# Decay and rate products on the array's two row halves, an own buffer for the short chunk's values, other orders at both ends, and PSUM scratch for inverses and decode

## The chip, the cores and the metric

The program runs on one core of a Trainium2 chip. The time is device microseconds from the launch to the end of one execution. Before the change it was 2742.42 us, the median of three runs (2741.14 to 2746.84).

## The reference

One inference step of a two-layer decoder: 16 meta tokens plus 1024 prompt tokens, and 8 further sequences with one token each, 1048 tokens in all, model width 1024. Layer 0 mixes tokens with a Conformer convolution, layer 1 with RWKV-7; each is followed by a squared-ReLU MLP of width 4096. Cut to what the change touches:

```python
def _rwkv7(h, shift_prev, S0, ...):                       # layer 1
    r = xr @ w_r; k = xk @ w_k; v = xv @ w_v              # xr.. = h + (previous h - h) * x_mix[i]
    w_log = -softplus(-(w0 + tanh(xw @ w1) @ w2)) - 0.5   # w1: 1024 x 64, w2: 64 x 1024: the decay
    decay = exp(-exp(w_log))
    a = sigmoid(a0 + (xa @ a1) @ a2)                      # a1: 1024 x 64, a2: 64 x 1024: the rate
    g = sigmoid(xg @ g1) @ g2
    # scan over the tokens, per head (64 x 64 state):
    #   sa = S @ -kk;  S = S * decay + sa (kk a)^T + v k^T;  y = S @ r
    out = ((group_norm(y) + bonus) * g) @ w_o
def _trunk(...):
    h = h + mixer(rmsnorm(h))                             # per layer
    h = h + square(relu(rmsnorm(h) @ w_mlp_in)) @ w_mlp_out
    return rmsnorm(h), conv buffers, shift rows, states   # the last 30 rows of each conv input are an output
```

## The kernel before

Activations lie with channels on the 128 partitions, eight blocks of 128 channels (KT = 8) by tokens. The tokens are cut into three groups of about 350 columns. Large products run in three passes: a weight is loaded as f32 (`pg_raw`), ScalarE casts it to `pg_hi` (L157), GpSimd subtracts to `pg_lo` (L162), and `mm3` (L187 to L189) adds hi\*hi, lo\*hi and hi\*lo. The RWKV projections (L891) are plain f32 matmuls, each of which shows as two records.

**Start.** `transpose_x` (L463) loads a group of x, squares and sums it on ScalarE (L437), takes the root (L438), transposes x (L470), and multiplies x by a diagonal matrix of 1/rms (L486, result `tn`). ScalarE (L488, `hn_h`) and VectorE (L489, `hn_l`) turn `tn` into the split activations, with norm weights from `pvec`, which `load_vecs` (L442) fills with small DMAs, a transpose and a copy (L453). `pw1` (L493) loads and splits the first conv weights (`pg`, `pa`) and multiplies (`ps_g`). Eight DMAs on ScalarE's queue (L1640) copy the old conv rows from one DRAM tensor to another.

**RWKV front.** Per group of tokens, `narrow` forms `p_wa`, in whose first 64 rows the decay's narrow product lies and in whose last 64 the rate's. `decay_rate` (L971) writes them to two 128-row tiles `lw` and `la` whose other halves hold constants (L807 to L809), and per head pair `lora2` (L981) multiplies the full 128 rows twice: `l_w` and `l_a` (L983). Values `vv` are transposed to `vt` (L1023, L1025) and written to DRAM (`d_v`, L1026). In the first group the 16 meta tokens, a short chunk, go the same way through `vm` (L1029, L1030), a tile with the same buffer tag as `vt`.

**Recurrence.** 17 chunks of 64 tokens. For a group of chunks `inverses` (L1159) loads blocks from DRAM into `ni`, runs 30 pairs of a product `tt` (L1172) and an add into `ni` (L1173) on VectorE, and writes them to DRAM (`d_p`). A chunk's `front` (L1186) loads `p` from there, transposes it to `x` on VectorE (L1203), and multiplies `A` (L1209), 64-row matmuls in pairs at `tile_position=(64 * q, 0)`. `chunk` (L1246) then begins with `gg` (L1257), which needs `x`, and `bT` (L1275).

**After the recurrence's first chunks.** Group 0's output projection (`ps_oo`, weights `wo`), its MLP (`m_h` L284, `m_l` L285, `ps_in`, `out`), the last chunks, and `norm_gate` for the later groups are interleaved. `filler` hands out generators by points: each `yield n` of a filling generator holds it back n points of the main stream. In this stage TensorE's instructions run in the order in which they are written (`in_order`); elsewhere the tile framework's scheduler orders every engine. `decode_step` (L1375) updates the states of the 8 single-token sequences on VectorE in 16 slices (`Sdec`, L1406 to L1414) beside group 0's MLP.

```python
nc.vector.tensor_mul(t4, S, overv(2))                             # L1406
nc.vector.tensor_reduce(sa[:, vs], t4, axis=AX.X, op=ALU.add)     # L1407
nc.vector.tensor_mul(S, S, overv(0))                              # L1408
nc.vector.tensor_mul(t4, overk(sa[:, vs]), overv(3))              # L1409
nc.vector.tensor_add(S, S, t4)                                    # L1410
nc.vector.tensor_mul(t4, overk(dq[:, 5, vs]), overv(1))           # L1411
nc.vector.tensor_add(S, S, t4)                                    # L1412
```

**End.** `final(g)` (L1552) squares the eight blocks, adds them into two tiles `acc_f` on GpSimd and VectorE (L230), sums over the channels with a matmul by ones (`fs`, L1569), transposes (`pf`, L1585), scales (L1588, L1590) and stores.

## Time and profile before

The profiled execution took 2743.3 us, of which the span between its first and last instruction is 2741.6 us: 1.7 us lie around it.

| what | us |
|---|---|
| median of three runs | 2742.42 |
| the profiled execution | 2743.3 |
| its span | 2741.6 |
| TensorE (PE) idle, total | 110.6 |
| VectorE (DVE) busy | 1727.8 |
| GpSimd (POOL) busy | 1455.6 |
| ScalarE (ACT) busy | 1124.0 |

The idle time is the span less the 2631.0 us in which PE was busy. A row of the timeline gives the start in us, the length of the stretch, the engine, the line, the operation, the output and inputs, shapes and the number of instructions in it; in brackets the idle time ahead of it and what ended it. A row of the windows gives, for a stretch of the span, its length and the busy time and count of each engine, then the granted TensorE clock (1.00 is full), DMA share and GB/s. A row of groups gives the line, operation, count, and after the bar the busy time and the mean ns of one.

### The profile page before, as it was taken

How to read it: one execution, taken by the hardware profiler on the slowest of the kernel's cores; microseconds unless marked ns; L12 is line 12 of the kernel's file. 1: busy time of each engine (PE TensorE's matmuls, PEld its weight loads, DVE VectorE, ACT ScalarE, POOL GpSimd, SP SyncE). 2: the span in 40 equal slices, each digit the busy share in tenths (PEclk: the TensorE clock that was granted, in tenths of full speed). 3: DMA queues.
4: the chain of work that ended last, by engine and by line, in shares of the span. 5: the costliest groups of instructions: out<-in, count | busy, mean ns of one | idle time of the engine just before them, and what ended most of it. 6: DMA issues, size and time to landing. Idle time of an engine off the chain costs nothing. (4 is left out here: it accounts for less than half of the span.)

```text
span 2741.6 us, 51590 instructions
## 1 busy us (share of the span) xinstructions
PE 2631.0 (96%) x19876; PEld 2489.7 (91%) x19876; DVE 1727.8 (63%) x3552; ACT 1124.0 (41%) x2097; POOL 1455.6 (53%) x2060
## 2 busy tenths in 40 slices
PE   8999999999999999998999999869998999999998
PEld 7999999999999999787887787768998999999998
DVE  5999999997445445335657466576679754334445
ACT  5546445445444333332434444434543542222223
POOL 6677878878887775022111113455677663333331
PEclk9999999999999999999999999989999999999999
DMA  6663544554456443667777768776675642222211
GB/s 182 170 185 113 163 138 125 158 174 131 142 159 192 138 139 101 184 198 198 202 189 203 189 166 196 192 192 163 176 234 165 166 130 87 66 69 70 70 55 43
DMA packets 624389, 412.30 MB, mean 150 GB/s; under 512 B 121656, under 2 KB 567288, under 8 KB 624142
## 3 DMA queue, kind: packets, MB, share of 16 engines
q1 hardware_dynamic: 543228, 358.60, 46.9%
q10 hardware_dynamic: 72386, 24.56, 4.2%
q0 software_dynamic: 8528, 25.83, 2.9%
q8 instruction: 157, 2.57, 0.4%
q14 instruction: 90, 0.74, 0.1%
HBM read 345.76 MB, written 64.07 MB: 149 GB/s over the span
## 5 line engine op out<-in xcount | busy, mean ns | idle before, releaser
L162 POOL TENSOR_TENSOR wo_lo<-wo_raw,wo_hi 128x256 fp32r<-128x256 f32 x736 | 546.7, 777 | 316.0 <-ACT wo_hi L157 314.2
L162 POOL TENSOR_TENSOR wi_lo<-wi_raw,wi_hi 128x256 fp32r<-128x256 f32 x640 | 472.1, 772 | 252.9 <-ACT wi_hi L157 244.4
L187 PE MATMUL out<-hh,wo_hi 128*128 128x352 f32 (+2 forms) x1536 | 501.5, 326 | 21.8 <-DVE h L354 12.8
L187 PE MATMUL ps_in<-m_h,wi_hi 128*128 128x352 f32 (+2 forms) x1536 | 494.3, 322 | 1.1 <-DVE h L354 1.1
L188 PE MATMUL out<-hh,wo_lo 128*128 128x352 f32 (+2 forms) x1536 | 495.2, 322 | 0.0
L189 PE MATMUL out<-hl,wo_hi 128*128 128x352 f32 (+2 forms) x1536 | 494.2, 322 | 0.0
L354 DVE TENSOR_TENSOR h<-h,out 128x352 f32<-128x352 f32 (+2 forms) x768 | 385.5, 510 | 171.7 <-PE out L189 170.1
L189 PE MATMUL ps_in<-m_l,wi_hi 128*128 128x352 f32 (+2 forms) x1536 | 492.2, 321 | 0.7 <-DVE m_l L285 0.7
L188 PE MATMUL ps_in<-m_h,wi_lo 128*128 128x352 f32 (+2 forms) x1536 | 491.8, 320 | 0.0
L524 DVE SCALAR_TENSOR_TENSOR cv<-u,wdw,cv 128x352 f32<-128x352 f32 (+2 forms) x720 | 377.8, 572 | 0.8
L157 ACT CAST wo_hi<-wo_raw 128x1024 fp32r<-128x1024 f32 x184 | 192.9, 1048 | 340.1 <-PE out L189 175.2
L157 ACT CAST wi_hi<-wi_raw 128x1024 fp32r<-128x1024 f32 x160 | 167.8, 1049 | 396.4 <-PE out L189 180.4
L187 PEld LDWEIGHTS out<-hh,wo_hi 128*128 128x128 f32 x1536 | 291.9, 190 | 27.9 <-DVE h L354 14.7
L188 PEld LDWEIGHTS out<-hh,wo_lo 128*128 128x128 f32 x1536 | 291.6, 190 | 0.8
L187 PEld LDWEIGHTS ps_in<-m_h,wi_hi 128*128 128x128 f32 x1536 | 289.4, 188 | 2.7 <-issue 1.3
L189 PEld LDWEIGHTS out<-hl,wo_hi 128*128 128x128 f32 x1536 | 290.5, 189 | 0.0
L189 PEld LDWEIGHTS ps_in<-m_l,wi_hi 128*128 128x128 f32 x1536 | 288.6, 188 | 1.9 <-DVE m_l L285 1.3
L188 PEld LDWEIGHTS ps_in<-m_h,wi_lo 128*128 128x128 f32 x1536 | 288.7, 188 | 0.9
L342 DVE SCALAR_TENSOR_TENSOR ps_in<-ps_in,rs_m 128x352 f32<-128x352 f32 (+2 forms) x192 | 100.2, 523 | 241.0 <-PE ps_in L189 240.6
L141 DVE TENSOR_TENSOR hl<-ps_in,hh 128x352 fp32r<-128x352 f32 (+2 forms) x192 | 98.6, 514 | 117.8 <-ACT hh L140 117.8
L343 ACT ACTIVATE ps_in<-ps_in 128x352 f32<-128x352 f32 (+2 forms) x192 | 85.0, 443 | 135.0 <-DVE ps_in L342 134.8
L1052 POOL DMA_DIRECT2D d_n<-n x32 | 24.6, 768 | 211.3 <-DVE n L1042 141.7
(361 smaller groups left out, 4823.3 us busy)
## 6 DMA issues: line engine op xcount, KB each, us to landing
wi_raw<-in_w_mlp_in_dram SPq DMA_DIRECT2D x160, 512.0 KB
wo_raw<-in_w_mlp_out_dram SPq DMA_DIRECT2D x160, 512.0 KB
wk_raw<-in_rwkv_w_k_dram SPq DMA_DIRECT2D x32, 512.0 KB
wr_raw<-in_rwkv_w_r_dram SPq DMA_DIRECT2D x32, 512.0 KB
wv_raw<-in_rwkv_w_v_dram SPq DMA_DIRECT2D x32, 512.0 KB
d_ab<-ab POOLq DMA_DIRECT2D x32, 512.0 KB, 4.6
pg_raw<-in_conv_w_pw_dram SPq DMA_DIRECT2D x24, 512.0 KB
pa_raw<-in_conv_w_pw_dram SPq DMA_DIRECT2D x24, 512.0 KB
```

The lines of the kernel that those rows point to most:

```text
L141: eng_lo.tensor_sub(lo, src, hi.bitcast(F32))
L157: nc.scalar.copy(hi[:, :a * b], raw[:, :a * b])
L162: eng_lo.tensor_sub(lo[:, cs], raw[:, cs], hi[:, cs].bitcast(F32))
L187: nc.tensor.matmul(ps, w[0], act[0], start=first, stop=False)
L188: nc.tensor.matmul(ps, w[1], act[0], start=False, stop=False)
L189: nc.tensor.matmul(ps, w[0], act[1], start=False, stop=last)
L342: nc.vector.scalar_tensor_tensor(s, s, 0.0, rs()[:, :n], op0=ALU.max, op1=ALU.mult)
L343: nc.scalar.activation(s, s, AF.Square)
L354: nc.vector.tensor_add(hv[:, 4 * i + m, :], hv[:, 4 * i + m, :], ps[:, :n])
L524: nc.vector.scalar_tensor_tensor(acc[m][:, :n], ug[:, m, j:j + n], wdw[:, m, j:j + 1], acc[m][:, :n], op0=ALU.mult, op1=ALU.add)
L1052: nc.gpsimd.dma_start(d_n[ch0:ch0 + ncg, p].rearrange("c r t -> r c t"), n32[:, :ncg])
```

## The change

The diff cut to what does work (arguments that only hand things through are left out):

```diff
+        nc.scalar.activation(eps_t[:, 3:4], eps_t[:, 0:1], AF.Sqrt)
...
             def transpose_x(g, ah, al, between=lambda: None):
                 n = G0[g][1]
+                staged = stage_vecs(0) if g == 0 else None
                 tiles = load_x(xin, g)
...
                 if g == 0:
-                    load_vecs([0])
+                    place_vecs(0, staged)
+                between()
...
+                    nc.sync.dma_start(o_conv_sample[0, m, 0:CB - 1, :], sd[m // 4][m % 4 * CB + 1:(m % 4 + 1) * CB])
...
-                for _ in transpose_x(0, *acts[0]):
-                    pass
+                first = pw1_weights(0, 0)
+                with tc.manual_schedule(engines={nc.scalar.engine}):
+                    for _ in transpose_x(0, *acts[0], lambda: ready.append(next(first))):
+                        pass
+                    ready.append(next(first))
...
-        lwa = [lorap.tile([P, N1], F32, name=f"l{b}") for b in "wa"]
-        for i, t in enumerate(lwa):
-            nc.scalar.copy(t[HALF[1 - i]], hsel[HALF[1 - i], 0:1].broadcast_to([HS, N1]))
+        lwa = lorap.tile([P, N1], F32, name="lwa")
...
-                        vm = pr.tile([P, 2, P], F32, name=nm("vm", p), tag="vt")
+                        vm = pr.tile([P, 1, P], F32, name=nm("vm", p), tag="vm")
...
-                for i, (t, b, nb, sign) in enumerate(((cum, "w", "w0", 0.5), (nav, "a", "a0", -0.5))):
-                    pl = lora2(wa2, p, lwa[i], f"{b}{p}")
+                pls = [bank(nm("l2", f"{b}{p}")) for b in "wa"]
+                for i, pl in enumerate(pls):
+                    nc.tensor.matmul(pl[:, :n], wa2[HALF[i], p, :], lwa[HALF[i], :n], start=True, stop=True, tile_position=(HS * i, 0))
+                for pl, t, nb, sign in zip(pls, (cum, nav), ("w0", "a0"), (0.5, -0.5)):
...
+            aside = bank(f"tt{c}", "x")[:B] if c + n == NCH else None
...
-                o = wk.tile([P, 256], F32, name=f"tt{c}_{j}", tag="tt")[:B, :j * wd].rearrange("p (s t) -> p s t", t=wd)
+                o = aside if aside is not None else wk.tile([P, 256], F32, name=f"tt{c}_{j}", tag="tt")[:B]
+                o = o[:, :j * wd].rearrange("p (s t) -> p s t", t=wd)
...
+        HOLD = 8
...
+            if c == NCH - 4:
+                yield HOLD
...
-                    t4 = rows(dk.tile([P, HV * HS], F32, name=f"t4{hv}", tag="t4"))
+                    t4 = rows(bank(f"t4{hv}", "x")[:, :HV * HS])
...
-                accs = mean_parts(hv, n, f"f{g}", True, "facc")
-                yield 3
+                if g:
+                    accs = [(actp, actp2)[g - 1].tile([P, cur["wide"]], F32R, name=f"fq{g}{k}", tag=f"acth{k}").bitcast(F32)
+                            for k in range(KT)]
+                else:
+                    accs = mean_parts(hv, n, f"f{g}", True, "facc")
+                    yield 3
                 for k in range(KT):
+                    if g:
+                        nc.scalar.activation(accs[k][:, :n], hv[:, k, :], AF.Square)
...
-                        nc.tensor.matmul(ps[:w, j:j + 1], acc[:, i:i + w], ones_d[:, 0:1], start=q == 0, stop=q == 1)
+                        nc.tensor.matmul(ps[:w, j:j + 1], acc[:, i:i + w], ones_d[:, 0:1], start=q == 0, stop=q == len(accs) - 1)
...
-                    if np_:
-                        nc.sync.dma_start(o_y_prompt[0, c:c + np_, :], ot[:np_, :])
+                        if np_:
+                            nc.sync.dma_start(o_y_prompt[0, c:c + np_, cs], ot[:np_, cs])
...
-            DL, DN = 74, 90
+            DL, DN, NL = 74, 90, 16
...
-                                ([late_start(DL), decode_step()], DL + DN), ([norm_gates(GN_OF[1]), ng2], NGA))
+                                ([late_start(DL), decode_step()], DL + DN), ([late_start(NL), norm_gates(GN_OF[1]), ng2], NGA + NL))
...
-            for q in range(DEC):
-                nc.scalar.dma_start(o_conv_sample[0, q, 0:CB - 1, :], state_conv[0, q, 1:CB, :])
```

So: the small vectors' loads are issued before those of x; a root is computed at the program's start, so that its table is loaded there; the first group's ScalarE work runs in written order, with the first `pg` split ahead of `hn_h` and the first `pa` split behind it; the eight DRAM copies are replaced by eight stores from tiles on chip, issued on SyncE's queue in the conv stage. Decay and rate sit in one tile `lwa`, and each pair of products is two 64-row matmuls at row positions 0 and 64 into two PSUM banks. `vm` has its own tag. The last group's `tt` and decode's `t4` lie in PSUM banks. Chunk 13 is held back by 8 points between its front and its first product, and the later norm gates start 16 points later. In the last two groups the squares go into the ones matmul without the adds, 24 matmuls a group for 6, and the outputs are stored by column halves.

ScalarE at the start, in the first group's `transpose_x`; `xj` is the squared x, `ss` its root, `hn_h` the split activation, `pg_0`, `pa_0`, `pg_1` conv weights. Before:

```order
L437 ACTIVATE xj_2_153,ss_2_154<-xt_2_151 96x1024
L157 CAST pg_0_hi<-pg_0_raw 128x1024
L1640 DMA out_dram<-in_state_conv_dram 16x1856 x2
L438 ACTIVATE ss_2_154<-ss_2_154,eps_t 96x1
L157 CAST pa_0_hi<-pa_0_raw 128x1024
L1640 DMA out_dram<-in_state_conv_dram 16x1856 x2
L157 CAST pg_1_hi<-pg_1_raw 128x1024
L1640 DMA out_dram<-in_state_conv_dram 16x1856
L488 ACTIVATE hn_h<-tn_0_216,pvec 128x352
L488 ACTIVATE hn_h<-tn_1_222,pvec 128x352
L488 ACTIVATE hn_h<-tn_2_228,pvec 128x352
```

After the change (line numbers are those of the changed kernel):

```order
L439 ACTIVATE ss_2_168<-ss_2_168,eps_t 96x1
L158 CAST pg_0_hi<-pg_0_raw 128x1024
L496 ACTIVATE hn_h<-tn_0_228,pvec 128x352
L496 ACTIVATE hn_h<-tn_1_234,pvec 128x352
L496 ACTIVATE hn_h<-tn_2_240,pvec 128x352
L496 ACTIVATE hn_h<-tn_3_246,pvec 128x352
L496 ACTIVATE hn_h<-tn_4_252,pvec 128x352
L496 ACTIVATE hn_h<-tn_5_258,pvec 128x352
L496 ACTIVATE hn_h<-tn_6_264,pvec 128x352
L496 ACTIVATE hn_h<-tn_7_270,pvec 128x352
L158 CAST pa_0_hi<-pa_0_raw 128x1024
L158 CAST pg_1_hi<-pg_1_raw 128x1024
```

All eight `hn_h` stand ahead of the casts of `pa_0` and `pg_1`, and the DRAM copies are gone.

TensorE where group 0's output projection is interleaved with chunk 13: `ps_oo0_6` and `ps_oo0_7` are its last two blocks, `ps_in1_0_0` to `ps_in1_2_0` the MLP's first three, `gg13` and `bT130` chunk 13's first products. Before:

```order
L188 MATMUL ps_oo0_6_20121<-z0_h7_19656,wo0_6_lo_19959 128x328
L189 MATMUL ps_oo0_6_20121<-z0_l7_19664,wo0_6_hi_19958 128x328
L1257 MATMUL gg13_20149<-x3213_19921,no13_19775 32x32 x16
L1275 MATMUL bT130_20173<-ident_58,bk13_19770 128x128 x4
L1275 MATMUL bT131_20179<-ident_58,bk13_19770 128x128 x4
L187 MATMUL ps_oo0_7_20189<-z0_h0_19649,wo0_7_hi_20064 128x328
```

After the change; the rows left out are the rest of `ps_oo0_7`, the statistics of the norm and the MLP's first three blocks:

```order
L190 MATMUL ps_oo0_6_20079<-z0_l7_19644,wo0_6_hi_19927 128x328
L188 MATMUL ps_oo0_7_20107<-z0_h0_19629,wo0_7_hi_20027 128x328
...
L189 MATMUL ps_in1_2_0_20267<-m10_h7_20142,wi1_0_2_lo_20259 128x328
L190 MATMUL ps_in1_2_0_20267<-m10_l7_20150,wi1_0_2_hi_20258 128x328
L1279 MATMUL gg13_20301<-x3213_19890,no13_19755 32x32 x16
L1297 MATMUL bT130_20325<-ident_58,bk13_19750 128x128 x4
L1297 MATMUL bT131_20331<-ident_58,bk13_19750 128x128 x4
L188 MATMUL ps_in1_3_0_20346<-m10_h0_20135,wi1_0_3_hi_20339 128x328
```

`gg13` has moved behind 100 more matmuls of 328 columns.

ScalarE at the last head pair of the first RWKV group: `vt0_7` and `vm0_7` are the transposed values of the long and the short chunks, `d_v` their place in DRAM, `r161` the key norm whose root it takes. Before:

```order
L1025 COPY vt0_7_13682<-vt0_7_13681 128x256
L979 ACTIVATE lg1_13626<-lg1_13626 128x256
L1026 DMA d_v_75<-vt0_7_13682 128x2x128
L1029 COPY vm0_7_13688<-vt0_7_13681 16x128
L921 ACT_TABLE_LOAD
L921 ACTIVATE r161_13756<-r161_13756 128x256
L1030 DMA d_v_75<-vm0_7_13688 16x128
L1067 COPY rk21_0_13782<-pr1_0_13743 128x256
```

After the change, where `sv` is the recurrence's first load of values from `d_v`:

```order
L1040 COPY vt0_7_13691<-vt0_7_13690 128x256
L1044 COPY vm0_7_13697<-vt0_7_13690 16x128
L994 ACTIVATE lg1_13635<-lg1_13635 128x256
L1041 DMA d_v_76<-vt0_7_13691 128x2x128
L1045 DMA d_v_76<-vm0_7_13697 16x128
L1262 DMA sv_12379<-d_v_76 64x8x64
L936 ACT_TABLE_LOAD
L936 ACTIVATE r161_13765<-r161_13765 128x256
```

The copy to `vm` now stands right behind that to `vt`, both stores follow, and a load from `d_v` has come ahead of the table load.

42 lines of the change are left out of this document (25 added, 17 removed).

## The prediction

> **What bounds the kernel now.** I read the busy shares first, then busy time by stage, then the list of what ended TensorE's waits, then the timeline around the longest of them.
>
> ```profile
> span 2741.6 us, 51590 instructions
> PE 2631.0 (96%) x19876; PEld 2489.7 (91%) x19876; DVE 1727.8 (63%) x3552; ACT 1124.0 (41%) x2097; POOL 1455.6 (53%) x2060
> 0.00:31.50 31.50, 18.66 (x93) 17.20 (x94) 9.49 (x28) 16.05 (x25) 17.18 (x32) 0.84 0.72 205
> 31.50:1100.00 1068.50, 1057.53 (x6611) 1044.74 (x6611) 794.02 (x1591) 495.67 (x767) 814.26 (x1145) 1.00 0.51 150
> 1100.00:1776.00 676.00, 643.63 (x6481) 535.84 (x6480) 370.77 (x882) 267.65 (x705) 138.01 (x255) 0.98 0.74 191
> 1776.00:1851.00 75.00, 48.88 (x485) 44.73 (x484) 51.22 (x108) 26.44 (x47) 41.60 (x50) 0.80 0.75 195
> 2027.00:2146.00 119.00, 104.83 (x663) 101.44 (x662) 116.56 (x235) 43.08 (x64) 93.50 (x112) 0.98 0.57 165
> 2146.00:2719.00 573.00, 572.12 (x3570) 569.54 (x3569) 261.51 (x474) 174.42 (x294) 240.11 (x326) 1.00 0.28 80
> 2719.00:2741.60 22.60, 13.55 (x100) 12.47 (x100) 11.98 (x25) 10.03 (x22) 2.98 (x3) 0.85 0.36 129
> ```
>
> TensorE is busy 96% of the span. The 110.6 us in which it is not lie unevenly: 12.8 in the first 31.5 us, 11 in the 1068 of layer 0, 32 in the RWKV front (1100 to 1776), 26 in the 75 us around chunk 13, 14 beside the decode step (2027 to 2146, where VectorE is busy 116.6 of 119 us), 0.9 in the 573 us of the last products, 9 at the end. So an edit pays in two ways only: fewer TensorE cycles, or a shorter wait of TensorE. The granted clock (next to last but two in a row) is low, 0.80 to 0.85, just where the waits are long; a wait avoided brings a little of that back as well.
>
> **The start: about -7.** What TensorE waits for ahead of its first large product:
>
> ```profile
> 12.84 4.23 PE L486 MATMUL tn<-dg,xt 128*128 128x128 f32 x30
> 18.88 1.04 ACT L157 CAST pa_hi<-pa_raw 128x1024 fp32r<-128x1024 f32 x1 [5.61 <-DMA pa_raw<-in_conv_w_pw_dram]
> 21.58 2.33 ACT L488 ACTIVATE hn_h<-tn,pvec 128x352 fp32r<-128x352 f32 x5
> 22.80 4.15 PE L486 MATMUL tn<-dg,xt 128*128 128x128 f32 x18 [5.72 <-DVE hn_l L489]
> 27.87 0.66 PE L187 MATMUL ps_g<-hn_h,pg_hi 128*128 128x352 f32 x1
> ```
>
> Five `tn` were done at 17.1, yet `hn_h` began at 21.58, since ScalarE stood at the cast of `pa_0`, whose weights landed at 18.88, then cast `pg_1`. TensorE stopped at its sixth `tn` (no bank free) for 5.72 us. With the new order `hn_h` runs from when `tn` and `pg_0` are there: eight at 2.33/5 = 0.47 us is 3.7 us, and `ps_g` follows the first `hn_h` and the first `tn` sequence instead of coming at 27.87. The 5.72 us wait goes; the DRAM copies no longer sit on ScalarE's queue; and the clock, half until 31.4 in these rows (`tn` 30 records in 4.23 us, then 18 in 4.15), may stay up. Gain 5.72 plus about 1.3 of clock: 7; ends 4 (the wait goes, but x or `pg_lo` is late next) and 10.5 (no half clock). After it TensorE is busy 1057.5 of 1068.5 us, so a gain here passes on if VectorE, 794 busy in that stage, does not set a place of it; that is why I don't take 10.5. The eight stores that replace the copies go to SyncE's queue in that stage, whose DMA share is 0.51: nothing, unless a weight load behind them is late.
>
> **Row halves: about -7.**
>
> ```profile
> L983 PE MATMUL l_w<-lw,wa x64: 379/386/796, 1146.9 to 1758.0; 128*128 128x256 f32 x32, 128*128 128x272 f32 x16, 128*128 128x264 f32 x16
> 1296.62 0.59 PE L983 MATMUL l_w<-lw,wa 128*128 128x256 f32 x2
> 1297.05 0.59 PE L983 MATMUL l_a<-la,wa 128*128 128x256 f32 x2
> 1297.48 2.75 PE L891 MATMUL pv<-mx,wv_raw 128*128 128x256 f32 x12
> 1300.17 1.16 PE L1209 MATMUL A<-xa,bk 64*128 64x128 f32 x16
> 1301.26 1.13 PE L891 MATMUL pv<-mx,wv_raw 128*128 128x256 f32 x4
> ```
>
> A product `l_w` takes 1297.05 - 1296.62 = 0.43 us, the pair 0.86. Each is two records, 64 over 32 products, and `l_a` has as many. No row shows this product on 64 rows, but `A` runs 64-row matmuls in pairs at positions 0 and 64: 16 records of 128 columns from 1300.17 to 1301.26, 1.09 us. One after the other they would be 16 x 0.215 / 2 = 1.72, two at a time 0.86; so they do run at once, with 0.23 us over. For a pair here that gives between 0.43 and 0.43 + 0.23 = 0.66; I take 0.55, a saving of 0.31 x 32 = 10 us, ends 6.4 (0.66) and 13.8. Some TensorE time freed in this stage turns into waits, since there 32 of 676 us are waits already, on ScalarE and VectorE chains that the change doesn't shorten. I let 0.7 pass: 7.
>
> The Trainium skill (TensorEngine Tiling (Array Packing), Tiling Modes) says that changing the tiling mode drains TensorE. By that rule the 64 switches that the change adds cost something each time. The `A` group, itself fenced by two such switches, came out 0.23 us over the ideal, so the trace agrees that there may be a price, and holds it under 0.23 us a pair; the sum by it would be the low end, 6.4.
>
> **The short chunk's own buffer: about -2.5.**
>
> ```profile
> 1276.89 0.26 ACT L1029 COPY vm<-vt 16x128 f32<-16x128 f32 x1 [9.85 <-DMA d_v<-vt]
> 1280.89 0.59 ACTq L1242 DMA_DIRECT2D sv<-d_v  x1
> 1285.28 1.22 PE L983 MATMUL l_w<-lw,wa 128*128 128x256 f32 x2 [5.22 <-ACT lw L973]
> ```
>
> ScalarE held still for 9.85 us at the last `vm`, because its buffer was still being written out as `vt`; behind it stood the root, and the tanh `lw` for which TensorE waited 5.22. With an own buffer the copy does not wait. But the new order puts a load `sv<-d_v` right behind the two stores and ahead of the root, and that load must wait for the stores to land: the same DMA that released `vm` at 1276.89. So ScalarE comes free no earlier than about 1276.9, and saves the later wait, from the root to 1280.89, which the second store then caused: 2 to 3 us. I take 2.5, ends 0 and 7 (the 5.22 and the half clock behind it). The seven other `vm` waits are not ahead of a TensorE wait. What is queued behind the new wait is the root, the casts `r16h` and `lw`, as before.
>
> **Chunk 13 and its inverse: about -12.**
>
> ```profile
> 1829.60 0.32 PE L189 MATMUL ps_oo<-z_l,wo_hi 128*128 128x328 f32 x1
> 1845.98 1.06 PE L1257 MATMUL gg<-x,no 32*32 32x32 f32 x32 [16.07 <-DVE x L1203]
> 1845.39 0.45 DVE L1203 STREAM_TRANSPOSE x<-p 128x256 f32<-128x256 f32 x1 [8.44 <-DMA p<-d_p]
> L1173 DVE TENSOR_TENSOR ni<-ni,tt 128x58 f32<-128x58 f32 (+14 forms) x29 | 15.1, 519 | 0.5
> L1172 DVE TENSOR_TENSOR tt<-ni 128x58 f32<-128x58 f32 (+14 forms) x29 | 13.6, 470 | 5.7 <-DMA ni<-d_n 5.1
> 1798.43 0.32 DVE L1173 TENSOR_TENSOR ni<-ni,tt 128x168 f32<-128x168 f32 x1
> 1830.33 0.74 DVE L1173 TENSOR_TENSOR ni<-ni,tt 128x168 f32<-128x168 f32 x1
> 1836.36 0.19 DVE L1173 TENSOR_TENSOR ni<-ni,tt 128x30 f32<-128x30 f32 x1
> ```
>
> The largest single wait: TensorE stood 16.07 us at `gg13`, for `x`, which came 9 us after the inverse's last add (1836.36), by way of a store and a load of `p`. With about 2.3 us of half clock behind it, it cost 18.4. Two edits bear on it. First, `gg13` moves behind 100 matmuls of 328 columns, 24 of them `ps_oo0_7`, at 0.15 us each: 15 us, and more with statistics and half clock. If that work can run, the wait is covered. But VectorE takes its instructions in order, and in the new order seven of the eight `m_l` of the MLP stand behind the transpose to `x`; so TensorE does `ps_oo0_7` (3.7 us) and then waits at the first MLP block for `m_l`, behind the same `x`. Second, the adds read `tt` from PSUM. The same add of 168 elements takes 0.32 us at 1798 and 0.74 at 1830, so the 29 adds would come from 15.1 to about 9.5 us if that goes, a gain of 5.6, and the order gives about 1. The products still read `ni` twice and keep their price. So `x` comes near 1839, not 1845.4, and `m_l` some 1 to 2 us later, against TensorE there at 1833.5: a wait of about 5 (bounds 0, if the whole inverse starts earlier, and 9, if the adds do not get faster), and 1.4 of clock. 18.4 - 6.4 = 12; ends 7 and 18.
>
> The Trainium skill (SBUF — State Buffer, Who interferes with whom) states that a DVE instruction with two SBUF inputs contends with a GpSimd instruction that reads SBUF, and one with at most one does not. The trace agrees, by the two rows of 168 elements.
>
> **Decode's scratch in PSUM: about -4.**
>
> ```profile
> L1410 DVE TENSOR_TENSOR Sdec<-Sdec,t 128x256 f32<-128x256 f32 x16 | 10.9, 682 | 0.2
> L1412 DVE TENSOR_TENSOR Sdec<-Sdec,t 128x256 f32<-128x256 f32 x16 | 11.1, 691 | 0.3
> L1414 DVE TENSOR_REDUCE yd<-t 128x4 f32<-128x256 f32 x16 | 6.6, 411 | 0.2
> L354 DVE TENSOR_TENSOR h<-h,out 128x328 f32<-128x328 f32 x56 | 26.7, 482 | 0.5 <-PE out L189 0.5
> L141 DVE TENSOR_TENSOR z_l<-zr,z_h 128x328 fp32r<-128x328 f32 x3 | 1.4, 490 | 0.0
> 2075.01 0.42 PE L187 MATMUL out<-hh,wo_hi 128*128 128x328 f32 x1 [2.15 <-DVE h L354]
> ```
>
> `L1410` and `L1412` would have one SBUF input and so come to the 0.41 us that the reduce of the same 256 elements takes: 22.0 - 32 x 0.41 = 8.9 us of VectorE, in the one stage where it is the bound and TensorE waits 14.2 us, on `h` and `hl`. An operand in PSUM is not dear here: `L354` reads one over 328 columns in 482 ns, `z_l` reads SBUF alone in 490. Against it, starting the norm gates 16 points later pushes some of their work into this stage: I put 4 to 5 us on VectorE. Net 4; ends -12 (the stage's waits nearly vanish) and +5 (gates outweigh it). What the gates feed stands behind them in the new order too, so they hold nothing else up.
>
> **The end: about -1.**
>
> ```profile
> 2730.56 0.53 DVE L230 TENSOR_TENSOR acc_f<-acc_f,sq_f 128x352 f32<-128x352 f32 x1 [0.22 <-ACT sq_f L225]
> 2731.14 1.17 PE L1569 MATMUL fs<-ones_d,acc_f 128*128 128x1 f32 x10
> 2735.73 1.07 SPq L1594 DMA_DIRECT2D out_dram<-ot  x1
> ```
>
> The adds ahead of the last `fs` go (0.53 and the step to PE), 18 one-column matmuls of 0.12 us are added per group, mostly ahead of the last square; the last output store starts with half a tile less ahead of it, but there are twice as many stores on SyncE's queue. -1, ends -2 and +1.5.
>
> **Sum:** -7 - 7 - 2.5 - 12 - 4 - 1 = -33.5, on the profiled execution's 2743.3: 2709.8. That execution lies 0.9 above the median of the runs, 2742.42, by which the sum is 2708.9; I say 2709.5.
>
> **Rivals.**
> 1. *The savings turn into other waits.* TensorE's freed time at the row halves is lost to ScalarE's and VectorE's chains (none passes), the start is taken back in layer 0 by VectorE, but for 1, and the decode stage nets nothing: -12 - 2.5 - 1 - 1 = -16.5, **2726**. For it: the RWKV front's waits are on chains (`lw`, `vv`, `rk`) that get no shorter. Against: TensorE's 643.6 of 676 us.
> 2. *All waits named vanish:* -10.5 - 13.8 - 5 - 18 - 10 - 2 = -59 at most, about -52 for most of it, **2690**. For it: ends are drawn from rows. Against: `x` still stands ahead of `m_l`.
> 3. *The row halves do not run at once*, as one would have it from the drain rule alone: their 7 goes, **2717**. The `A` group speaks against.
> 4. *VectorE pays for PSUM scratch (slower).* Per slice of decode eight of nine instructions read or write `t4`, 128 in all, in the stage where VectorE is full; 58 more lie on the inverse's chain. If none gets faster and each costs c more, decode grows by 128c and `x` comes 58c later. With c = 0, chunk 13 still gains 4.4: `x` at 1844.4 by the order, `m_l` at 1846, against TensorE at 1833.5, is a wait of 12.5 with 1.5 of clock, for 18.4 before. The rest, start, row halves, `vm` and end, gains 17.5. So it is slower from 186c = 21.9, c = 0.12 us; at c = 0.16 it is **2750**. Against it speak `L354` and `z_l`, 482 and 490 ns.
>
> **Numbers.** Forecast 0.56, rival 1 0.21, rival 2 0.12, rival 3 0.04, rival 4 0.07. The forecast's own ends, with terms rarely all at one side, are 2697 and 2721; taking in rival 1 and half of rival 2 the range is 2691 to 2730. About 0.2%, 5.5 us, is what a measurement can tell from no change. Faster by more: 0.56 + 0.20 + 0.11 + 0.03 = 0.90 less a little for misjudged terms, 0.88; within 0.2%: 0.05; slower: 0.07.
>
> **What would show it.** Right: the first `ps_g` near 20; from one `l_w` pair to the next product 0.45 to 0.65 us; `vm` with no wait on `d_v`; the wait ahead of `gg13` gone and one of about 5 us at the MLP's first block, released by `m_l`; the 29 `L1173` near 9.5 us together, `L1410` and `L1412` near 410 ns each; VectorE below 113 of 119 us beside decode. Wrong: pairs at 0.86 us; `L1409` or `L1410` above 700 ns; layer 0 that grows by what the start won; new waits of TensorE on `rk` or `vv` in the RWKV front.

## The result and the profile after

The changed kernel takes 2750.71 us (median of 13 runs, 2746.44 to 2754.96), the kernel before, run beside it, 2748.09 (13 runs, 2741.14 to 2761.67): a ratio of 1.001 (95% interval 0.9998 to 1.0022), so no gain, where 33 us were forecast. The profiled execution took 2749.91 us, its span is 2748.2.

First the page of the changed kernel, its span and busy time; then its windows, cut at eight instructions of TensorE that both kernels have. Columns as before: length, busy time and count on PE, PE's weight loads, DVE, ACT and POOL, granted clock, DMA share, GB/s.

```profile
span 2748.2 us, 51718 instructions
PE 2641.3 (96%) x19948; PEld 2480.3 (90%) x19948; DVE 1716.6 (62%) x3546; ACT 1122.1 (41%) x2095; POOL 1443.8 (53%) x2054
...
0.00:228.03 228.03, 218.65 (x1396) 214.41 (x1396) 193.68 (x406) 122.70 (x199) 160.73 (x250) 1.00 0.63 175
228.03:463.23 235.20, 214.38 (x1313) 209.75 (x1314) 207.54 (x418) 107.84 (x174) 170.99 (x235) 0.96 0.43 127
463.23:1797.15 1333.92, 1291.18 (x10518) 1160.92 (x10516) 777.05 (x1682) 550.46 (x1131) 643.48 (x957) 0.99 0.62 170
1797.15:1875.41 78.26, 65.24 (x561) 60.23 (x561) 58.56 (x119) 32.11 (x59) 44.89 (x58) 0.86 0.74 192
1875.41:2152.07 276.66, 268.18 (x2505) 257.51 (x2504) 217.44 (x450) 128.91 (x228) 195.74 (x246) 0.99 0.72 198
2152.07:2220.90 68.83, 66.74 (x414) 64.74 (x413) 40.78 (x56) 37.48 (x68) 51.32 (x65) 1.00 0.56 156
2220.90:2732.76 511.86, 509.67 (x3182) 505.74 (x3181) 217.90 (x413) 138.32 (x231) 176.70 (x248) 1.00 0.22 65
2732.76:2748.20 15.44, 7.22 (x71) 6.97 (x69) 3.67 (x9) 4.24 (x9) 0.00 (x0) 0.75 0.33 114
```

The same stretches in both kernels, each from one instruction of TensorE to another, in us. "Forecast" is the term of the sum that falls there.

| stretch | before | after | difference | forecast |
|---|---|---|---|---|
| launch to layer 0's first `ps_o` | 235.21 | 228.03 | -7.2 | -7 |
| to the last `pw` (the conv's decode rows, layer 0) | 212.09 | 235.20 | **+23.1** | 0 |
| to group 0's first `ps_oo` (rest of layer 0, RWKV front) | 1334.49 | 1333.92 | -0.6 | -9.5 |
| to the first `out` of group 0's MLP (chunk 13) | 90.42 | 78.26 | -12.2 | -12 |
| to the last `out` of that MLP (decode) | 287.69 | 276.66 | -11.0 | -4 |
| to the end of group 1's projection | 61.75 | 68.83 | +7.1 | 0 |
| to the last `out` | 505.66 | 511.86 | +6.2 | 0 |
| to the end | 14.29 | 15.44 | +1.1 | -1 |
| sum | 2741.6 | 2748.2 | **+6.6** | -33.5 |

So 31 us were won in four stretches, and 37.5 given back in the other four. In the second stretch TensorE is busy 214.4 of 235.2 us: 21 us of idle time that were 1.4 before. That stretch was priced at nothing. The same stretch of the kernel before, and below it that of group 1's projection, where TensorE was never idle (windows):

```profile
235.21:447.30 212.09, 210.66 (x1313) 207.50 (x1314) 206.46 (x419) 108.53 (x175) 171.52 (x235) 1.00 0.47 136
2159.90:2221.65 61.75, 61.75 (x394) 61.71 (x393) 33.98 (x53) 37.02 (x67) 52.86 (x65) 1.00 0.62 172
```

### The profile page after: what moved, and what is told of

Its sections match the earlier page's. It is cut to its first block, busy times and chain, and to the rows that moved or that the text cites. A ratio compares the mean times of both kernels' runs of the same rounds, so it can differ in the third digit from the quotient of the medians.

```text
span 2748.2 us, 51718 instructions
## 1 busy us (share of the span) xinstructions
PE 2641.3 (96%) x19948; PEld 2480.3 (90%) x19948; DVE 1716.6 (62%) x3546; ACT 1122.1 (41%) x2095; POOL 1443.8 (53%) x2054
## 5 line engine op out<-in xcount | busy, mean ns | idle before, releaser
L536 DVE SCALAR_TENSOR_TENSOR cv<-u,wdw,cv 128x348 f32<-128x348 f32 (+2 forms) x720 | 377.9, 574 | 0.7
L906 PE MATMUL pv<-mx,wv_raw 128*128 128x256 f32 (+2 forms) x512 | 133.1, 406 | 6.7 <-ACT rk L1082 4.7
```

Source lines behind the costliest of these rows:

```text
L536: nc.vector.scalar_tensor_tensor(acc[m][:, :n], ug[:, m, j:j + n], wdw[:, m, j:j + 1], acc[m][:, :n], op0=ALU.mult, op1=ALU.add)
L906: nc.tensor.matmul(ps[:, :n], w[:, k, :], act[k], start=k == 0, stop=k == KT - 1)
```

## The experiments

Each kernel below is the changed kernel or the kernel before with the edits named; the code is cut to those edits. Ratios are to the kernel before, run beside each on the same chip. The second stretch of the table took 216.2 us in `best1_nl0` and 211.0 in `best2`, one kernel twice, so a kernel that ran once settles only what its trace shows locally.

### What the eight stores do

The timeline of the changed kernel around the gap in layer 0, engines mixed (start, length, engine, line), then two of its windows:

```profile
301.35 14.54 SPq L564 DMA_DIRECT2D out_dram<-sdec  x4
316.00 7.01 SPq L147 DMA_DIRECT2D wo_raw<-in_w_mlp_out_dram  x2
335.49 1.04 ACT L158 CAST wo_hi<-wo_raw 128x1024 fp32r<-128x1024 f32 x1 [17.35 <-DMA wo_raw<-in_w_mlp_out_dram]
337.88 0.66 PE L559 MATMUL pw<-ident,sdec 120*128 120x120 f32 x2 [14.85 <-ACT win L561]
...
308.00:314.00 6.00, 6.00 (x39) 6.00 (x39) 2.87 (x7) 0.00 (x0) 1.62 (x4) 1.00 0.06 26
323.00:337.00 14.00, 0.03 (x1) 0.00 (x0) 0.18 (x1) 1.51 (x3) 0.39 (x1) 0.50 0.45 139
```

While four stores of 29 rows are being issued, SyncE stands at them 14.54 us, and the window from 308 shows a DMA share of 0.06, one of 16 engines, and 26 GB/s. The packets say the same: each 4096-byte row took 159 ns, one after the other, which is 4.6 us for 29 rows and 37 us for all eight stores. The weights `wo` are issued behind them; ScalarE waits 17.35 us for them, and TensorE, whose work is ordered behind that cast, stands. One rival would be that the bytes alone delay the weights: 0.95 MB would need 6 us at the 159 GB/s that `stores_28` reaches below. Another is that SyncE's queue is the wrong place. The kernels move the stores to ScalarE's or GpSimd's queue, put the old copies back, or keep the stores on SyncE and cut only their shape:

```diff
 # stores_act: nc.scalar, stores_pool: nc.gpsimd
-nc.sync.dma_start(o_conv_sample[0, m, 0:CB - 1, :], ...)
+nc.scalar.dma_start(o_conv_sample[0, m, 0:CB - 1, :], ...)
 # copies_back: no such store, and as in the kernel before
+for q in range(DEC):
+    nc.scalar.dma_start(o_conv_sample[0, q, 0:CB - 1, :], state_conv[0, q, 1:CB, :])
 # stores_28: 28 rows and 1 row
+r0 = m % 4 * CB + 1
+for a, b in ((0, CB - 2), (CB - 2, CB - 1)):
+    nc.sync.dma_start(o_conv_sample[0, m, a:b, :], sd[m // 4][r0 + a:r0 + b])
```

> The changed kernel, with the eight stores of the old conv rows issued by GpSimd instead of SyncE, all else as changed. Theory Q (queue order): in the changed kernel each store of 29 rows runs at some 25 GB/s, which is about what one of the 16 DMA engines moves, and the MLP's weight loads stand behind the stores on SyncE's queue; off that queue the 14.85 us wait ahead of pw and the 2.6 us ahead of out vanish, layer 0 ends 20 to 24 us earlier and the span falls from 2748 to about 2726. Rival E (engine): the stores hold a DMA engine that every weight load also needs a share of, so the loads are late whichever queue issues the stores: span 2740 to 2748. Rival S (start): the gap comes from the earlier start meeting the conv stage in another phase, not from the stores: span unchanged, 2748.

> The changed kernel, with the eight stores issued by ScalarE. When GpSimd issued them, two things changed at once: they left SyncE's queue, and their rows no longer ran one behind the other but many at a time, so that one store landed in 4.6 us at the median. Here they leave SyncE's queue but, as far as ScalarE's queue works as SyncE's does, still run row by row, 159 ns for 4096 bytes, 232 rows, 37 us. Theory Q (only the order on the queue matters): the 14.85 us wait ahead of pw goes, layer 0 ends 18 to 24 us earlier than in the changed kernel, span 2726 to 2732. Rival E (the one DMA engine that carries them is also needed by each weight load): loads in that stretch stay late by about half, layer 0 ends 0 to 12 us earlier, span 2737 to 2748. A risk of its own: ScalarE stands at the issue of a store, up to some us each.

> The changed kernel, with the eight stores taken out and the eight DRAM-to-DRAM copies of the kernel before put back in their old place. Theory Q and rival E both: the gap of about 23 us in layer 0 goes; up to 2 us of the start's gain of 7 may go back to the copies on ScalarE's queue: span 2725 to 2728, time against before about 0.993. Rival S: the gap stays, span about 2748.

> The changed kernel, with each store of 29 rows cut in two, 28 rows and one row, both still issued by SyncE in the same place. In the traces so far a transfer of 30 rows of 4096 bytes ran its rows side by side (30 within 1 us), while those of 29 rows and a load of 31 rows, whichever queue issued them, ran one row after the other at 159 ns and more. Theory E (one DMA engine carries all rows of such a transfer, and weight loads that need it wait): 28 rows are spread again, the 14.85 us wait ahead of pw goes with nothing moved to another queue, layer 0 ends 18 to 24 us earlier than in the changed kernel, span 2725 to 2731. Rival Q (what matters is that stores stand ahead of the loads in SyncE's queue): twice as many stores stand there, the gap stays, span 2746 to 2754.

| kernel | us (median, range, runs) | ratio, 95% interval |
|---|---|---|
| stores_pool | 2731.62 (2726.91 to 2737.61, 5) | 0.9944 (0.9925 to 0.9963) |
| stores_act | 2752.7 (1) | none |
| copies_back | 2733.66 (2729.28 to 2741.99, 6) | 0.9955 (0.9939 to 0.9971) |
| stores_28 | 2728.86 (2725.78 to 2729.6, 4) | 0.9927 (0.991 to 0.9943) |

`stores_28` from the view of its DMA issues in time, and its window at the place of the one above:

```profile
295.85 3.11 SPq L566 DMA_DIRECT2D out_dram<-sdec  x6
...
308.00:314.00 6.00, 6.00 (x40) 5.98 (x40) 6.00 (x15) 2.71 (x6) 5.12 (x8) 1.00 0.55 159
```

The same bytes on the same queue at the same place, 28 rows and one row in place of 29, and the gap is gone: six of its sixteen stores issue in 3.11 us, and the DMA engines run at 159 GB/s. The second stretch of the table takes 211.1 us, 1 less than in the kernel before. Neither the queue nor the bytes are the cause, but that 29 rows go to one engine. `stores_act` shows it from the other side (its timeline):

```profile
298.64 8.15 ACTq L564 DMA_DIRECT2D out_dram<-sdec  x1
306.85 10.92 ACTq L564 DMA_DIRECT2D out_dram<-sdec  x2
...
306.52 15.94 SPq L147 DMA_DIRECT2D wo_raw<-in_w_mlp_out_dram  x2
```

The stores are still serial, and now hold up ScalarE (8.15 and 10.92 us), and SyncE's weight loads with them: two take 15.94 us to issue, though no store stands ahead of them on SyncE's queue. The second stretch takes 236.5 us, so none of the 23 us is won back. On GpSimd's queue the rows are spread: a store takes 3.9 to 5.0 us from issue to landing, and the gap is gone, though that stretch, 217.4 us, is still 5 above the kernel before.

The Trainium skill (DMA: Bandwidth & Descriptors, Why a DMA increments its semaphore by 16 and not by 1) states how many engines a transfer is given: the largest count up to 16 that divides the slowest dimension of both sides, with an exception for GpSimd's queue. By it 29 and 31 rows get one engine and 28 rows get 14. The trace agrees for 29 rows, a DMA share of 0.06, which is one of 16; that 28 rows get just 14 no run here shows.

Two more kernels ask whether the kernel before could have had this gain alone: it, with its DRAM copies on GpSimd's queue, and it, with the eight stores from GpSimd in place of the copies.

```diff
 # b_copies_pool (kernel before)
-    nc.scalar.dma_start(o_conv_sample[0, q, 0:CB - 1, :], state_conv[0, q, 1:CB, :])
+    nc.gpsimd.dma_start(o_conv_sample[0, q, 0:CB - 1, :], state_conv[0, q, 1:CB, :])
 # b_stores_pool (kernel before): no copies, in conv_dec
+nc.gpsimd.dma_start(o_conv_sample[0, m, 0:CB - 1, :], sd[m // 4][m % 4 * CB + 1:(m % 4 + 1) * CB])
```

> The kernel before, with only the eight DRAM-to-DRAM copies issued by GpSimd in place of ScalarE. Theory C (the copies hold ScalarE at the start): ScalarE's first hn_h moves from 21.6 to 18 to 19 us and ps_g from 27.9 to 23 or 24, with no other part of the change; layer 0 ends 3 to 5 us earlier; span about 2737. Rival O (the order of the casts ahead of hn_h, as I argued): hn_h still stands behind the cast of pa_0 whose weights land at 18.9, so ps_g comes at 26 to 28; span 2740 to 2742.

> The kernel before, with the eight DRAM-to-DRAM copies replaced by stores of the rows from the tiles on chip, issued by GpSimd in the conv stage; nothing else of the change. ScalarE's order at the start is the old one, with the casts of pa_0, pg_1 and here pa_1 as well ahead of the first hn_h. Theory C (what the start won was the copies' absence, on ScalarE's queue and from the DMA engines): ps_g comes near 22, as in the changed kernel, and layer 0 ends 4 to 6 us earlier. Theory O (it was the new order): hn_h waits for the last of the three weights, ps_g comes at 25 to 28 and layer 0 ends within 2 us of before. Span 2736 to 2738 by C, 2740 to 2743 by O.

Neither gains: 1.0005 (0.9995 to 1.0016) and 1.001 (0.9995 to 1.0024), 10 runs each. On the copies they decide nothing, since in both the scheduler used the free queue to send another transfer first; the timeline of `b_stores_pool`:

```profile
0.81 0.55 ACTq L457 DMA_DIRECT2D wst<-in_conv_w_dw_dram  x1
11.46 1.30 PE L470 MATMUL tx<-ident,xt 128*128 128x128 f32 x5 [11.46 <-DMA xt<-in_x_prompt_dram]
```

`wst` has 31 rows. Sent ahead of x, it holds the first transpose to 11.46 (11.27 in `b_copies_pool`), which began at 5.74 in the kernel before. The DMA packets of `b_stores_pool` show how: 334 of the 352 rows of x have started by 7.9 us, and the last 18 start one by one from 8.63 to 13.76, between the rows of `wst`, which run from 1.77 to 12.25. So a second odd shape delays another queue's transfer, here without any copies or stores beside it.

### The start: order or copies

`copies_back` has the new order and the old copies. `start_free` (on `best3`, below) has no copies, and leaves the order of ScalarE to the scheduler again:

```diff
-with tc.manual_schedule(engines={nc.scalar.engine}):
+with ExitStack():
```

> As best3, with ScalarE at the start ordered by the scheduler as before the change, so that the casts of pa_0, pg_1 and pa_1 stand ahead of the first hn_h; the copies stay out, and the 31-row load stays behind that of x. Theory O (the order matters): hn_h waits for the third and fourth weight block and ps_g comes at 25 to 28 where it is near 21 in best3. Theory C (only the copies mattered): ps_g comes within 1 us of best3.

Timelines: ahead of the first `ps_g` in the changed kernel, then one row of `copies_back`, then one of `start_free`:

```profile
17.92 4.07 ACT L496 ACTIVATE hn_h<-tn,pvec 128x352 fp32r<-128x352 f32 x8 [5.82 <-PE tn L494]
21.94 0.43 PE L188 MATMUL ps_g<-hn_h,pg_hi 128*128 128x352 f32 x1
```

```profile
22.22 2.33 ACT L496 ACTIVATE hn_h<-tn,pvec 128x352 fp32r<-128x352 f32 x5 [7.92 <-DMA out_dram<-in_state_conv_dram]
```

```profile
20.11 1.04 ACT L158 CAST pg_hi<-pg_raw 128x1024 fp32r<-128x1024 f32 x1 [5.97 <-DMA pg_raw<-in_conv_w_pw_dram]
```

With the copies back, ScalarE is held 7.92 us by the copies, `hn_h` begins at 22.22 and `ps_g` at 28.09. Without the copies but with the old order, ScalarE stands at a cast, and `ps_g` comes at 29.03. With both edits it comes at 21.94, and in `best3` at 22.37. So both are needed for the gain of 7; neither alone brings `ps_g` forward (27.87 in the kernel before). `start_free` took 2717.07 us in its one run, 5 more than `best3`.

### Row halves: the edges

`pair_twice` repeats the two products. If 64-row products ran one after the other, a second pair would add 0.86 us; if they run at once and a fixed price stands at the edges, it adds 0.43.

```diff
-for i, pl in enumerate(pls):
+for i, pl in list(enumerate(pls)) * 2:
```

> The changed kernel, with each pair of row-half products issued twice in a row into the same two banks (same values, written over), 64 64-row matmuls more. Read: from the record ahead of the pair to the second record behind it, 1.26 us in the changed kernel against 1.29 before. Theory D (edges): the pair itself runs two at a time, and what eats the gain is a fixed 0.1 us at each change between 128-row and 64-row tiling or ahead of the first weights, about four of them; the second pair then adds only 0.43 to 0.45 us. Rival H (half rate): each 64-row pass takes 0.32 us instead of 0.216 whatever stands beside it: the second pair adds 0.64. Rival N (not at once): it adds 0.86. Span against the changed kernel: +12 to +14 by D, less where TensorE waits anyway; +18 by H; +25 by N.

The kernel that ran also had the DRAM copies back, so it compares with `copies_back`. TensorE's timeline at one pair: changed kernel, kernel before, and `pair_twice`.

```profile
1348.50 0.59 PE L998 MATMUL l_g<-lg,wg 128*128 128x256 f32 x2
1349.03 0.48 PE L1096 MATMUL l_w<-lwa,wa 64*128 64x256 f32 x1
1349.04 0.48 PE L1096 MATMUL l_a<-lwa,wa 64*128 64x256 f32 x1
1349.35 0.38 PE L1096 MATMUL l_w<-lwa,wa 64*128 64x256 f32 x1
1349.36 0.38 PE L1096 MATMUL l_a<-lwa,wa 64*128 64x256 f32 x1
1349.66 0.92 PE L906 MATMUL pv<-mx,wv_raw 128*128 128x256 f32 x3
```

```profile
1349.43 0.59 PE L983 MATMUL l_g<-lg,wg 128*128 128x256 f32 x2
1349.87 0.59 PE L983 MATMUL l_w<-lw,wa 128*128 128x256 f32 x2
1350.30 0.59 PE L983 MATMUL l_a<-la,wa 128*128 128x256 f32 x2
1350.73 0.81 PE L891 MATMUL pv<-mx,wv_raw 128*128 128x256 f32 x3
```

```profile
1340.14 0.60 PE L997 MATMUL l_g<-lg,wg 128*128 128x256 f32 x2
1341.73 1.35 PE L905 MATMUL pv<-mx,wv_raw 128*128 128x256 f32 x5
```

The halves do run at once: starts lie 0.01 us apart. But from the start of `l_g` to the end of the third `pv` record is 2.08 us (1349.66 + 0.92 - 1348.50) against 2.11 before (1350.73 + 0.81 - 1349.43). Ahead of the pair the step from `l_g` is 0.53 us, where it was 0.44; the first pass takes 0.32 and the second 0.31, where 0.22 each would be free of price; and three `pv` records take 0.92 behind it, where they took 0.81. About 0.1 us is lost at each of these four places, 0.4 of the 0.43 us that were saved. It is so at every pair: over the 16 pairs of 256 columns, the median from the last `l_g` record to the second `pv` record is 1.262 us, and 1.295 before. In `pair_twice` `pv` begins 1.59 us after `l_g`, where it is 1.16 above: the second pair adds 0.43, with no new edge. So the price is fixed, and doesn't come from the products.

The total alone would not have told this. From the first `l_w` to the last, `pair_twice` takes 630.7 us and `copies_back` 611.4, 19 more, near the 18 expected of the half rate. But at 25 of the 32 places the second pair adds 0.37 to 0.46 us, 11 in all, where the half rate would add 0.64 at each; the rest falls at the seven places where TensorE waits between these records.

On `best3` the pair was put back to 128 rows (`lora2` and the tiles `lw`, `la` of the kernel before):

```diff
-lwa = lorap.tile([P, N1], F32, name="lwa")
+lwa = [lorap.tile([P, N1], F32, name=f"l{b}") for b in "wa"]
```

> As best3, with the decay and rate products as before the change: 128 rows each, two tiles with constant halves. Theory D: at 1.26 us against 1.29 us from the record ahead to the second behind, the row halves save 32 x 0.03 = 1 us, so the two kernels are the same within 3 us and from first to last l_w within 2 us. Rival, my forecast: without them it is 7 to 10 us slower.

2713.53 us (2712.03 to 2715.14, 4 runs) against 2711.86 for `best3`, spans 2710.3 and 2710.2. From the first `l_w` to the last it is 611.5 us against 608.6, and 611.1 in the kernel before against 610.1 in the changed one. The row halves are worth 0 to 3 us, not the 7 of the forecast.

### Chunk 13 and decode: which edit won what

Three kernels undo one edit each on `best1_nl0` (below): `gg13` at its old place, `tt` back in SBUF, and decode's `t4` back in SBUF.

```diff
 # hold0
-if c == NCH - 4: yield HOLD
 # tt_sbuf
+aside = None
 # t4_sbuf: t4 as a tile of dk, in SBUF
```

> As best1_nl0, with chunk 13 no longer held back by 8 points, so that TensorE's order has gg13 where it was before, right behind ps_oo0_6; tt stays in PSUM. Theory: x is ready 5 to 7 us earlier than in the kernel before, by the faster adds and the order of VectorE's work, so the wait ahead of gg is 9 to 11 us where it was 16.07, and from the first ps_oo to the first ps_in it is 60 to 63 us, against 51.1 with the hold and 71.5 before. Rival: the hold does nothing that the faster adds don't do alone; then the wait at gg is 3 to 5 us and the stretch is 52 to 55 us.

> As best1_nl0, with the inverses' tt of the last group back in SBUF; the hold stays. Theory: the 29 adds into ni go back from about 10 to about 15 us together, x comes 5 us later, and the wait at the first MLP block, behind x, grows by 4 to 6 us: first ps_oo to first ps_in unchanged, first ps_in to first out longer by 4 to 6. Rival: the adds were slowed by something else (the norm gates' work standing between them), so they stay near 10 us and nothing changes.

> As best1_nl0, with decode's t4 back in SBUF. Theory: the two adds of a slice go back from 0.41 to about 0.69 us, 9 us of VectorE in the stage that it bounds, and the second half of group 0's MLP (out 384 to its end) takes 8 to 12 us longer, near the 130.7 us of before; span +8 to +12. Rival: VectorE's gain was in the gates' later start alone (which is undone in both here): no change within 2 us.

From the first `ps_oo` to the end, one profiled execution each: 938.2 us in `best1_nl0`, 941.5 in `hold0`, 940.4 in `tt_sbuf`, 951.6 in `t4_sbuf`. Five executions with the same code in this part (`best1_nl0`, `best2`, `best3`, `rows_full`, `start_free`) take 937.0 to 939.6. So `t4` in PSUM is worth 13; the move's 3 and the 2 of `tt` in PSUM hardly stand out at this end, though their waits do. Rows of `hold0` (timeline), `tt_sbuf` and `t4_sbuf` (groups, the part with the inverse and the part with decode):

```profile
1828.04 1.06 PE L1277 MATMUL gg<-x,no 32*32 32x32 f32 x32 [6.29 <-DVE x L1222]
```

```profile
L1192 DVE TENSOR_TENSOR ni<-ni,tt 128x30 f32<-128x30 f32 (+14 forms) x30 | 14.6, 485 | 0.5
```

```profile
L1432 DVE TENSOR_TENSOR Sdec<-Sdec,t 128x256 f32<-128x256 f32 x16 | 11.4, 715 | 0.2
```

Alone, each edit of chunk 13 takes most of the wait away: with the faster adds, `gg13` at its old place waits 6.29 us, not 16.07; with the move and slow adds, the first `ps_in` comes 55.8 us after the first `ps_oo`, against 51.05 with both and 71.5 before. The 6.29 lies between the two expectations, and the time that `tt_sbuf` loses lies ahead of the first `ps_in`, not behind it as expected. The gains don't add, since both edits shorten one wait.

### The tail

Two edits were suspected of slowing the last 580 us: the new final norm, and the norm gates held back 16 points. `final_old` (on `copies_back`) takes the final norm of the kernel before; `best1` has stores from GpSimd and that norm; `best1_nl0` also starts the gates early; `best2` is the same kernel in four runs; `best3` has the 28-row stores on SyncE, the old final norm and the early gates.

```diff
 # final_old: in final(g), for all three groups
+accs = mean_parts(hv, n, f"f{g}", True, "facc")
+yield 3
 # best1_nl0, best2, best3
-DL, DN, NL = 74, 90, 16
+DL, DN, NL = 74, 90, 0
```

> As copies_back, with the last norm of the kernel before as well (squares added into two tiles, 6 matmuls by ones for a group, whole output stores). Theory F: of the 14 us that the changed kernel loses after group 0's MLP, some 8 come from the last norm: 72 one-column records more at 0.09 us, 34 of them alone on TensorE at the very end; so from group 1's first projection to the end it is 6 to 9 us shorter than in copies_back, span 2718 to 2721. Rival G: the loss is VectorE and ScalarE work of the norm gates that the later start pushes into group 1's projection; then the old end changes it by +1 to -2 us, span 2725 to 2728.

> The changed kernel, with the eight stores issued by GpSimd and the last norm of the kernel before. Theory: the two corrections add, since they lie 1400 us apart: stores on GpSimd gave a span of 2729.9, the old last norm takes 7 to 11 off: 2719 to 2723, ratio to before about 0.991. Rival: TensorE's time at the start (6 us, which came with the copies off ScalarE's queue) is lost in layer 0, where VectorE is full, so the result is no better than copies put back plus the old norm, 2720.8.

> As best1, with the later norm gates started as early as in the kernel before (0 points in place of 16). Theory G: the gates' late start is what costs 7 to 10 us in group 1's projection, so that stretch shrinks to what it was before (61.6 us), while VectorE's work ahead of it grows: the wait at gg for chunk 13 comes back in part, and the decode stage gives back some; span within 4 of best1, either way. Rival P: the 7 to 10 us are last-norm and statistics products moved there from later, paid back afterwards: the stretch stays at 68 to 71 us and the span is within 2.

> The same kernel as best1_nl0 (stores issued by GpSimd, the old last norm, norm gates as early as before), now timed: 2717 to 2721, ratio to before 0.988 to 0.992, and the wait ahead of pw absent again. If the late gates don't matter, it equals best1, 2722.

> The changed kernel with three corrections: the stores cut into 28 rows and one row on SyncE's queue, the old last norm, the norm gates as early as before. Theory: like best2, with the stores off GpSimd, which in the conv stage is busy with weight splits: layer 0 ends 0 to 5 us earlier, 2712 to 2718, ratio to before 0.987 to 0.990. Rival: sixteen stores on SyncE hold the weight loads up a little where eight on GpSimd did not: 2718 to 2722.

| kernel | last `out` of group 0's MLP to the end, profiled | us (median, range, runs) | ratio, 95% interval |
|---|---|---|---|
| before | 581.7 | 2748.09 (2741.14 to 2761.67, 13) | 1 |
| after | 596.1 | 2750.71 (2746.44 to 2754.96, 13) | 1.001 (0.9998 to 1.0022) |
| copies_back | 596.2 | 2733.66 | 0.9955 |
| final_old | 592.3 | 2726.9 (2719.95 to 2730.55, 6) | 0.9924 (0.9908 to 0.994) |
| stores_pool | 597.8 | 2731.62 | 0.9944 |
| best1 | 589.1 | 2722.11 (2718.4 to 2727.01, 5) | 0.9909 (0.9895 to 0.9924) |
| best1_nl0 | 584.7 | 2718.5 (1) | none |
| best2 | 585.7 | 2717.36 (2709.16 to 2719.6, 4) | 0.9882 (0.9864 to 0.99) |
| best3 | 585.4 | **2711.86** (2705.49 to 2712.44, 4) | **0.9862 (0.9847 to 0.9877)** |

The new final norm costs 4 us of the tail on `copies_back` and 9 on `stores_pool`; the late gates cost another 4 (589.1 to 584.7). They bought nothing earlier: from the first `ps_oo` to the last `out` of that MLP takes 354.7 us in `best1` and 353.5 in `best1_nl0`. Of the 14.4 us that the tail grew, some 4 (585.4 against 581.7) are left in `best3`. `hold0`, which is `best1_nl0` without the move of chunk 13, shows where they come from: its tail is 582.0, that of the kernel before. Its row for group 1's projection, and below it that of `best1_nl0` (windows):

```profile
2134.31:2196.12 61.81, 61.81 (x394) 61.77 (x393) 33.68 (x55) 37.48 (x68) 53.27 (x66) 1.00 0.61 171
2132.03:2197.94 65.91, 65.47 (x411) 64.19 (x410) 34.91 (x57) 38.25 (x70) 49.71 (x64) 1.00 0.60 168
```

With the move 17 more records run on TensorE in this stretch, of statistics and final transposes (`st_m`, `pf`) that come later without it. So the 8 points by which chunk 13 is held back also shift what is interleaved behind it, and cost 4 us there and 3 to 4 of the tail, by one execution of `hold0`. `best3` is faster than both kernels, by 1.4% against the kernel before.

## Why the prediction was wrong, point by point

**The stores: the step that failed.** The prediction said of the eight stores: "nothing, unless a weight load behind them is late". It named the right condition and dismissed it by the stage's mean DMA share of 0.51. A mean share says what bandwidth is left, not how many engines one transfer gets. The loads were late by 17 us, the price was 23 us, and cutting the shape of the stores alone brought the median to 2728.86. No rival had it: rival 4's 2750 was close to the result by another mechanism, dearer PSUM scratch, which the rows below refute.

By the table, the result lies 40 us above the forecast: 23 from the stores, 9 from the RWKV front (the row halves, above all), 15 from the tail, less 7 that decode won beyond its term.

**The start: right in size and in mechanism**, -7.2 for -7, and `ps_g` at 21.94 for "near 20"; the prediction named both the new order and the copies, and both were needed.

**Row halves: a term mis-sized, by its whole size.** The mechanism held (at once, 0.01 us apart), the saving of 0.31 us a pair did not: it measured 0.03. I read the `A` group from its first start to the start of the next product, and took 0.23 us over the ideal for the whole price. That reading holds two of the four edges and leaves out two, which the same trace has: the last `pv` record ahead of the group starts 0.31 us before it, and the first behind it is followed after 0.32, where a `pv` record takes 0.22. Counting all four gives about 0.4 us a pair, what the changed kernel shows. The rival of the drain rule (2717) was the right one of the two here, though its reason, that the halves don't run at once, was wrong.

The Trainium skill (TensorEngine Tiling (Array Packing), Tiling Modes) states that changing the tiling mode drains TensorE. The trace agrees that a change costs time, 0.1 us at each of the four places; the bound that the prediction drew from the `A` group was too low. At the price measured here the gain is near 0, and not the 6.4 that the prediction put beside that rule.

**The short chunk's buffer: as said.** The timeline of the changed kernel:

```profile
1295.47 1.28 ACT L936 ACT_TABLE_LOAD   x1 [11.29 <-DMA d_v<-vm]
1301.14 0.79 PE L1096 MATMUL l_w<-lwa,wa 64*128 64x256 f32 x1 [3.41 <-ACT lwa L988]
```

The wait has gone from `vm` to the table load, behind the new load's wait for the stores, as worked out; TensorE waits 3.41 us and not 5.22: -1.8 for -2.5.

**Chunk 13: right in size and in mechanism, but for a price behind it.** Timeline and groups of the changed kernel:

```profile
1853.38 0.45 DVE L1222 STREAM_TRANSPOSE x<-p 128x256 f32<-128x256 f32 x1 [1.52 <-DMA p<-d_p]
1855.45 0.42 PE L190 MATMUL ps_in<-m_l,wi_hi 128*128 128x328 f32 x1 [2.82 <-DVE m_l L286]
...
L1191 DVE TENSOR_TENSOR tt<-ni 128x30 f32<-128x30 f32 (+14 forms) x30 | 15.6, 521 | 4.6 <-DMA ni<-d_n 3.9
L1192 DVE TENSOR_TENSOR ni<-ni,tt 128x30 f32<-128x30 f32 (+14 forms) x30 | 9.7, 322 | 0.7
```

The adds come to 9.7 us for the 9.5 worked out, the products keep their price, `x` comes 56.2 us after the first `ps_oo` (63.6 before), the wait ahead of `gg13` is gone, and the one at the MLP's first block is 2.82 us for "about 5". The stretch gave 17.5 up to that wait and 5.3 back when `gg13` and its like ran behind it. The 4 us that the move costs in group 1's projection were in no term.

**Decode: the mechanism right, the size too small.** Groups of the changed kernel in the part with decode:

```profile
L1432 DVE TENSOR_TENSOR Sdec<-Sdec,t 128x256 f32<-128x256 f32 x16 | 6.6, 413 | 0.2
L1434 DVE TENSOR_TENSOR Sdec<-Sdec,t 128x256 f32<-128x256 f32 x16 | 6.6, 413 | 0.1
```

413 ns, as forecast, 8.8 us of VectorE. I took 4 to 5 us of it away for gates pushed into the stage. They were not pushed there but into the tail: the stretch gained 11.0, and `t4_sbuf` loses 13.

**The end: wrong in sign, and the tail was left out.** The forecast was -1 for the end and nothing for the tail ahead of it. The tail grew by 14.4, by the final norm, the late gates and the move of chunk 13. Groups and timeline of the changed kernel:

```profile
L1597 PE MATMUL fs<-ones_d,fq 128*128 128x1 f32 (+1 forms) x96 | 10.6, 230 | 0.0
...
2736.17 3.43 PE L1597 MATMUL fs<-ones_d,fq 128*128 128x1 f32 x34
```

Groups 1 and 2 have 48 `fs` records each, where they had 12: 36 more and not 18, and 34 of them stand alone at the end, 3.43 us, not "ahead of the last square". The prediction counted 18 more matmuls a group as 18 records, though each shows as two.

**The sum.** With the stores cut to 28 rows, the old final norm and early gates, the kernel lands at 2711.86, near the 2709.5 of the forecast. That is luck and no proof of its terms: the row halves' missing 7 us are made up by decode's 7.

## What to carry to other kernels

Before a transfer is called free because the DMA engines have room, count its rows: 29 and 31 rows, which no number from 2 to 16 divides, ran on one engine here and held transfers behind them and on another queue; the stores of 29 rows cost 23 us in layer 0, which a cut into 28 + 1 rows took away. A short switch of the array's tiling paid its price at the edges, so read a candidate from the record ahead of it to the second record behind it; here one pair gained next to nothing, and a second pair in the same mode took 0.43 us where two full products take 0.86. Work that is held back in or pushed out of a full stage has to be followed to the stage where it lands.

## What the runs showed of the hardware that was not expected

A transfer of 29 rows ran row by row, 159 ns for 4096 bytes, about 26 GB/s, and such a transfer, of 29 or of 31 rows, delayed those of other queues too (`stores_act`, `b_stores_pool`).

Changing between two tilings of the array cost about 0.1 us at each of the four edges of a pair, and a second pair in the same mode only its own 0.43 us.

An add of two SBUF tiles on VectorE, usually 0.5 us, took 9.09 while GpSimd went from one instruction to the next without a pause (timeline of the changed kernel):

```profile
2214.33 9.09 DVE L261 TENSOR_TENSOR acc_m<-sq,sq 128x352 f32<-128x352 f32 x1 [0.18 <-ACT sq L250]
2213.72 5.62 POOL L163 TENSOR_TENSOR wi_lo<-wi_raw,wi_hi 128x256 fp32r<-128x256 f32 x8
2219.30 0.95 POOL L261 TENSOR_TENSOR acc_m<-acc_m,sq 128x352 f32<-128x352 f32 x1
2220.21 2.83 POOL L163 TENSOR_TENSOR wi_lo<-wi_raw,wi_hi 128x256 fp32r<-128x256 f32 x4
```

The add spans some dozen of GpSimd's instructions, so it was not held by one of them alone; that they held it is inferred from the times. The kernel before has a stall of 8.66 us of the same kind, at an `m_l`. What it costs was not tried.
